# A two-layer decoder trunk on one core: more products on zeros, another order for the first rounding, and the small inputs on ScalarE's queue

## The chip, the cores and the metric

The kernel runs on one core of one Trainium2 chip. The metric is the device time of one execution in microseconds (us); the figure for a kernel is the median of its runs. One execution of the kernel before was also taken with the hardware profiler, and every view below is of that execution.

A core has TensorE (PE in the profile, with PEld for its weight loads), VectorE (DVE), ScalarE (ACT), GpSimd (POOL), and SyncE (SP), which here only issues transfers. Each engine runs its own instructions in the order of the program; an instruction whose operands are not ready holds up all that stand behind it on that engine.

## The reference, cut to what matters

```python
D_MODEL, SEQ, DEPTH, HEAD_DIM = 1024, 512, 2, 64
def fox_moba_layer(x, norm_g, w_in, ...):         # layer 0
    h = rms_norm(x, norm_g)
    proj = h @ w_in                               # 1024 x 4104 columns
    # split: q,k,v of 8 forgetting heads, their forget logits, q,k,v of 8 MoBA heads, gate
    out_a = fox_attention(...); out_b = moba_attention(...)
    mix = concatenate([out_a, out_b])
    return x + (mix * silu(gate)) @ w_out
def conformer_conv_layer(x, ...):                 # layer 1
    val, glu_gate, z = split(rms_norm(x, norm_g) @ w_in, 3)
    u = depthwise_causal_conv(val * sigmoid(glu_gate), width=31) + conv_b
    return x + (silu(layer_norm(u)) * silu(z)) @ w_out
```

All is in float32. Layer 0 starts with the product of the normalised tokens, 512 x 1024, with the columns of `l0_w_in`.

## The kernel before, in words

Products in float32 are made of three products of rounded operands: a tensor `a` is kept as `hi` (rounded to TensorE's fp32r) and `lo = a - hi`, and `a @ w` is `hi·whi + lo·whi + hi·wlo`. The tokens' two halves are `hhi` and `hlo`, the weights' `whi` and `wlo`. The weights come in 36 chunks of 256 columns (1 MB each); chunk `i` is loaded into one of two buffers `wst` by `fetch(i)` and rounded by `split(i)` (`split_w`, L162 to L179): `whi` by ScalarE (L173), `wlo` by VectorE or GpSimd (L177), each in four pieces of two of the eight contraction steps k. For chunk 0 GpSimd makes the first and third piece of `wlo`, VectorE the second and fourth.

The start of the kernel, in the order of the code:
- `small_parts` (L200) loads the small inputs of layer 0 (norm gains, rope tables, biases; 90 KB) in one transfer on SP's queue (L203) to the tile `parts`.
- SP then loads the first token tile of the transposed input (`xt`, 128 tokens, in two halves, L218), the four quarters of weight chunk 0 (L152), the other three token tiles, and the untransposed rows `xs` with the weight chunks 1 and 2 between and behind them.
- TensorE does `WARM` = 11 products on a tile of zeros, `idle` (L313), whose result is never read.
- For each token tile `t` and each half of its channels: VectorE multiplies by the norm's gain (`hn`, which shows as `v`, L328), ScalarE rounds that to `hhi` (L330), VectorE subtracts to get `hlo` (L331). After tile 0 the code calls `split(0)`.
- For each tile ScalarE squares `xs` and sums it (L337), VectorE scales the sum (`vv`, L339) and GpSimd takes the power, which gives `rinv` (L340): the norm's factor, applied when a product is read out (L386, L388). `spread_rinv` transposes `rinv` on TensorE (L345).
- Chunk 0 (`qk_chunk(0)`) is the first real product: 24 matmuls for each of four token tiles (L360), all `whi·hhi` first, then `whi·hlo`, then `wlo·hhi`. Tile 0 and 1 write the banks `mm`, tile 2 and 3 the banks `s`. Chunk 1 writes `mm`, `mm`, `st` and `o`; chunk 2 follows.

The code is not in the final order: a scheduler of the language simulates the program and orders the instructions of each engine by their simulated times. `tc.issue_after(x)` holds the instructions under it back, in that order, until `x` has been placed. So a change at the start can alter the order of everything behind it.

Of the kernel before, what the change touches and what calls it, by code (L numbers as in the profile page):

```python
# [57 lines left out]
def SPLIT_ENG(i, nc):  # L58

    if i in DMAS:  # L60
        return None
    return nc.gpsimd if i in PSPLIT else nc.vector
# [20 lines left out]
KO = 4  # L83
KORD = (6, 0, 1, 2, 4, 5, 7, 3)
SPR = 1
WARM = 11
WARM2 = 2
HP = None
HP1 = None
# [5 lines left out]
def tile_kernel(ctx: ExitStack, tc: tile.TileContext, x, xt, w, small0, small1, l1_norm, out):  # L95
# [7 lines left out]
    V, A, G, T, SY = nc.vector, nc.scalar, nc.gpsimd, nc.tensor, nc.sync  # L103
# [20 lines left out]
    def mmbank():  # L124
        turn[0] += 1
        return stbank() if l1p and turn[0] % 3 == 0 else bank("mm", 2)
# [7 lines left out]
    def bc_row(src, n, parts=P):  # L134
        return bass.AP(tensor=src.tensor, offset=src.offset, ap=[[0, parts], [1, n]])
# [19 lines left out]
    def split_w(w, ring, eng, parts, cast):  # L155
        st, n = w
        if ring == "late":
            lo = l1p[0].tile([P, KC * WC], F32R, tag="gh", name="lo", bufs=1)
            lo = lo.rearrange("p (k n) -> p k n", k=KC)
            A.activation(lo, st, AF.Copy, scale=-1.0)  # L160
            G.dma_start(lo.bitcast(F32), st, accum_op=ALU.add)
            return None, lo  # L162
        if ring == "main":
            hi, lo = flat(main, F32R, "whi", n, 2), flat(main, F32R, "wlo", n, 2)
        else:
            hi, lo = (flat(l1p[0], F32R, "wx", n, 4, WC) for _ in range(2))
        m = KC // parts
        if cast:
            G.dma_start(hi, st)
        for k in range(0, KC, m):  # L170
            ks = slice(k, k + m)
            if not cast:
                A.activation(hi[:, ks], st[:, ks], AF.Copy)  # L173
            if eng is None:
                A.activation(lo[:, ks], st[:, ks], AF.Copy, scale=-1.0)
            else:
                (V if eng is G and parts == 4 and k % 4 and V0 else eng).tensor_tensor(lo[:, ks], st[:, ks], hi[:, ks].bitcast(F32), op=ALU.subtract)  # L177
        if eng is None:
            G.dma_start(lo.bitcast(F32), st, accum_op=ALU.add)  # L179
        return hi, lo  # L180
# [16 lines left out]
    tab = so.tile([P, 2, NT, 4, 16], F32, name="tab")  # L197


    def small_parts(src, sizes, pool):  # L200
        n = sum(m for _, m in sizes)
        t = pool.tile([P, n], F32, name="parts")
        SY.dma_start(t, src)  # L203
        r, o = {}, 0
        for name, m in sizes:
            r[name] = t[:, o:o + m]
            o += m
        return r

    parts0 = small_parts(small0, SIZES0, consts)  # L210
    xts = []
    for t in range(NT):
# [18 lines left out]
    def split(i):  # L231
        if i < len(wsrc):
            wts[i] = split_w(raw.pop(i), rings[i], SPLIT_ENG(i, nc), APARTS if i in DMAS else 4 if i == 0 or 17 <= i < 24 else WPARTS, i in CAST)
# [77 lines left out]
    pw = mmbank()  # L311
    for _ in range(WARM):
        T.matmul(pw, idle[:, :P], idle, start=True, stop=True)  # L313
# [9 lines left out]
    for t in range(NT):  # L323
        hn = v0[:, (t % 2) * KC * P:(t % 2 + 1) * KC * P].rearrange("p (k t) -> p k t", k=KC)
        ts = slice(t * P, (t + 1) * P)
        for h in range(2):
            ks = slice(h * 4, h * 4 + 4)
            V.tensor_tensor(hn[:, ks], xts[t][:, ks], gcol[:, ks, None].to_broadcast([P, 4, P]),  # L328
                            op=ALU.mult)
            hp[2 * t + h] = hpart = A.activation(hhi[:, ks, ts], hn[:, ks], AF.Copy)  # L330
            V.tensor_tensor(hlo[:, ks, ts], hn[:, ks], hhi[:, ks, ts].bitcast(F32),  # L331
                            op=ALU.subtract)
        if t == 0:
            split(0)
    for t in range(NT):
        with tc.issue_after(hp[JO[t]].ins):
            A.activation(xs[t], xs[t], AF.Square, accum_out=ssx[:, t:t + 1])  # L337
# [347 lines left out]
    l1 = ctx.enter_context(tc.tile_pool(name="l1", bufs=1, reuse_waits="tile"))  # L685
# [4 lines left out]
    gh = l1.tile([P, 2, D], F32, tag="gh", name="gh", bufs=1)  # L690
    grow1, hn1 = gh[:, 0], gh[:, 1]
    SY.dma_start(grow1, bc_row(l1_norm, D))
    parts1 = small_parts(small1, SIZES1, l1)
    cw = parts1["conv_w"].rearrange("p (k w) -> p k w", k=KC)
    V.tensor_scalar(cw, cw, 0.5, None, op0=ALU.mult)
    cbias, lng, lnb = parts1["conv_b"], parts1["ln_g"], parts1["ln_b"]
# [427 lines left out]
SIZES1 = (("conv_b", KC), ("ln_g", KC), ("ln_b", KC), ("conv_w", KC * CONV))  # L1124
# [62 lines left out]
```

## Time and profile before

| | us |
|---|---|
| median of 3 runs | 524.99 (523.45 to 526.51) |
| the profiled execution, its own time | 525.7 |
| its span, first to last instruction | 523.9 |
| PE busy | 505.9 (97% of the span) |
| DVE, ACT, POOL busy | 375.8, 329.8, 232.3 |

The mean granted clock of TensorE was 0.984. A matmul's end is modelled in the trace and its start is not, so a PE that is shown as busy may still be slowed: the count of matmuls in a stretch and the clock tell how fast it ran. Rows of a timeline have start, duration, engine, line, operation, operands and count, and in brackets the idle time before and what ended it. Rows of a table of stretches have, for each stretch, the busy time of PE, PEld, DVE, ACT and POOL with the number of instructions, the granted clock, the share of the 16 DMA engines in use and GB/s.

### The profile page before, as it was taken

The page shows a single profiled execution, that of the slowest core. Times are in us where ns is not written, and L with a number is a line of the kernel's source. Part 1 is how long each engine was busy: PE and PEld are TensorE (multiplying, and loading weights), DVE is VectorE, ACT ScalarE, POOL GpSimd, SP SyncE. Part 2 cuts the span into 40 slices and gives each one's busy share as a digit, 9 for nine tenths or more (in the row PEclk, how much of TensorE's full clock was granted, in tenths as well). Part 3 has the DMA queues.
Part 4 walks back from the last instruction along what each step waited for, and adds up shares of the span by engine and source line. Part 5 has one row for each costly group of instructions (what it writes and reads, how often), then busy time and mean ns, then how long its engine had stood idle before and what let it go on. Part 6 is the DMA issues. An engine that isn't in the chain of part 4 may idle for free.

```text
span 523.9 us, 9734 instructions
## 1 busy us (share of the span) xinstructions
PE 505.9 (97%) x3683; PEld 462.0 (88%) x3683; DVE 375.8 (72%) x788; ACT 329.8 (63%) x668; POOL 232.3 (44%) x255
## 2 busy tenths in 40 slices
PE   6999999999999999999999999999999999779997
PEld 3999998987889988788779999999999887559997
DVE  6856577856565587586696256999999997778741
ACT  3846687876555785576374735998686755478230
POOL 4166545010323143223202113879998875777200
PEclk8999999999999999999999999999999999879999
DMA  7742222202122233303219578488999799962111
GB/s 264 306 180 83 81 81 102 76 30 82 61 102 81 81 125 99 138 10 114 102 41 398 124 213 233 89 210 290 230 305 255 203 261 314 265 171 101 41 49 43
DMA packets 16566, 79.05 MB, mean 151 GB/s; under 512 B 1988, under 2 KB 4352, under 8 KB 8712
## 3 DMA queue, kind: packets, MB, share of 16 engines
q1 hardware_dynamic: 12776, 51.17, 26.8%
q0 software_dynamic: 3744, 27.26, 21.7%
q8 instruction: 29, 0.48, 0.4%
q14 instruction: 17, 0.14, 0.1%
HBM read 50.07 MB, written 2.14 MB: 100 GB/s over the span
## 4 chain that ended last, share of the span: by engine, by line
PE 72%; DMA 12%; DVE 5%; ACT 5%; POOL 3%; issue 2%; SPq 0%; POOLq 0%; ACTq 0%
PE mm L360 30%; DMA wst<-in_w_dram 7%; PE mm L369 6%; PE mm L370 6%; PE mm L371 6%; PE st L360 4%; PE o L602 3%; PE tp L525 3%; POOL pacc L775 2%; PE o L360 2%; PE s L509 2%; DMA lo<-wst 2%; PE s L511 2%; DMA wlo<-wst 2%; DMA wx<-wst 2%
## 5 line engine op out<-in xcount | busy, mean ns | idle before, releaser
L775 POOL TENSOR_TENSOR pacc<-pacc,tm 128x256 f32<-128x256 f32 (+1 forms) x125 | 120.2, 982 | 16.3 <-ACT tm L774 10.5
L765 DVE SCALAR_TENSOR_TENSOR s<-u,parts,s 128x256 f32<-128x256 f32 (+1 forms) x211 | 108.2, 571 | 0.5
L360 PE MATMUL mm<-whi,hhi 128*128 128x256 f32 (+1 forms) x352 | 100.2, 292 | 3.1 <-ACT hhi L330 2.9
L360 PE MATMUL mm<-whi,hlo 128*128 128x256 f32 (+1 forms) x352 | 99.4, 289 | 0.0
L360 PE MATMUL mm<-wlo,hhi 128*128 128x256 f32 (+1 forms) x352 | 99.0, 289 | 0.0
L774 ACT ACTIVATE tm<-u,parts 128x256 f32<-128x256 f32 (+1 forms) x125 | 66.2, 571 | 14.7 <-POOL pacc L775 14.2
L360 PEld LDWEIGHTS mm<-whi,hhi 128*128 128x128 f32 x352 | 66.9, 193 | 4.7 <-ACT hhi L330 3.4
L360 PEld LDWEIGHTS mm<-whi,hlo 128*128 128x128 f32 x352 | 66.7, 193 | 0.2
L360 PEld LDWEIGHTS mm<-wlo,hhi 128*128 128x128 f32 x352 | 66.6, 193 | 0.2
L173 ACT ACTIVATE whi<-wst 128x512 fp32r<-128x512 f32 (+2 forms) x77 | 49.3, 707 | 8.8 <-DMA wst<-in_w_dram 7.8
L522 ACT ACTIVATE p<-p,nm 128x128 f32<-128x128 f32 (+3 forms) x64 | 35.8, 559 | 26.9 <-DVE nm L521 26.3
L517 POOL TENSOR_TENSOR cb<-cb,mask 128x128 f32<-128x128 f32 x32 | 15.4, 485 | 77.4 <-DVE nm L521 48.8
L177 POOL TENSOR_TENSOR wlo<-wst,whi 128x512 fp32r<-128x512 f32 (+1 forms) x22 | 31.0, 1417 | 38.3 <-ACT whi L173 38.3
L177 DVE TENSOR_TENSOR wlo<-wst,whi 128x512 fp32r<-128x512 f32 (+1 forms) x50 | 40.4, 840 | 9.9 <-ACT whi L173 9.8
L369 PE MATMUL mm<-nhi,wx 128*128 128x256 f32 (+1 forms) x104 | 33.8, 325 | 0.0
L371 PE MATMUL mm<-nhi,wx 128*128 128x256 f32 (+1 forms) x104 | 32.9, 316 | 0.0
L370 PE MATMUL mm<-nlo,wx 128*128 128x256 f32 (+1 forms) x104 | 32.8, 316 | 0.0
L370 PE MATMUL mm<-nlo,whi 128*128 128x256 f32 (+1 forms) x104 | 31.9, 307 | 0.0
L369 PE MATMUL mm<-nhi,whi 128*128 128x256 f32 (+1 forms) x104 | 31.8, 307 | 0.0
L371 PE MATMUL mm<-nhi,wlo 128*128 128x256 f32 (+1 forms) x104 | 31.7, 306 | 0.0
L395 POOL TENSOR_TENSOR rq<-vq,mhalf 128x16 f32<-128x16 f32 x8 | 26.2, 3281 | 5.0 <-DVE vq L393 4.9
L525 PE MATMUL tp<-identf,p 128*128 128x128 f32 x160 | 28.1, 275 | 0.4 <-ACT pt L533 0.3
(292 smaller groups left out, 1434.8 us busy)
## 6 DMA issues: line engine op xcount, KB each, us to landing
wst<-in_w_dram SPq DMA_DIRECT2D x33, 1024.0 KB, 5.2
wx<-wst POOLq DMA_DIRECT2D x13, 1024.0 KB, 7.9
wlo<-wst POOLq DMA_DIRECT2D x8, 1024.0 KB, 8.9
whi<-wst POOLq DMA_DIRECT2D x3, 1024.0 KB, 5.9
wst<-in_w_dram SPq DMA_DIRECT2D x2, 1040.0 KB, 4.7
xs<-in_x_dram SPq DMA_DIRECT2D x4, 512.0 KB, 9.4
cb<-cdram SPq DMA_DIRECT2D x8, 256.0 KB, 3.7
x<-in_x_dram SPq DMA_DIRECT2D x4, 512.0 KB, 7.2
```

Source lines behind the costliest of these rows:

```text
L173: A.activation(hi[:, ks], st[:, ks], AF.Copy)
L177: (V if eng is G and parts == 4 and k % 4 and V0 else eng).tensor_tensor(lo[:, ks], st[:, ks], hi[:, ks].bitcast(F32), op=ALU.subtract)
L360: T.matmul(po, a[:, k, ts], b[:, k, :n], start=first and i == 0, stop=last and i == len(prods) - 1)
L369: T.matmul(po, whi[:, k, cs], a, start=k == 0, stop=False)
L370: T.matmul(po, whi[:, k, cs], b, start=False, stop=False)
L371: T.matmul(po, wlo[:, k, cs], a, start=False, stop=k == KC - 1)
L395: G.tensor_tensor(r, v, mhalf[:, :16].rearrange("p (t h) -> p t h", t=NT), op=ALU.pow)
L522: A.activation(p[:, :w], p[:, :w], AF.Exp, bias=nm, scale=-1.0, accum_out=sm[:, h, t:t + 1])
L525: T.transpose(tp[:, j * P:(j + 1) * P], p[:, j * P:(j + 1) * P], identf)
L765: V.scalar_tensor_tensor(acc[:, o], v, w, first[0][:, :n] if i == 1 else acc[:, o], op0=ALU.mult, op1=ALU.add)
L774: A.activation(tm[:, :n], v, AF.Copy, scale=w)
L775: G.tensor_tensor(pacc[:, o], pacc[:, o], tm[:, :n], op=ALU.add)
```

## The change

It has three parts. `WARM` goes from 11 to 22. `small_parts` issues on ScalarE's queue unless told otherwise, and layer 1's call names SP's queue, so only the load at the start moves. `split(0)` is held back until the second rounding of tile 0 has been placed.

```diff
-WARM = 11
+WARM = 22
...
-    def small_parts(src, sizes, pool):
+    def small_parts(src, sizes, pool, queue=None):
         n = sum(m for _, m in sizes)
         t = pool.tile([P, n], F32, name="parts")
-        SY.dma_start(t, src)
+        (A if queue is None else queue).dma_start(t, src)
...
         if t == 0:
-            split(0)
+            with tc.issue_after(hpart.ins):
+                split(0)
...
-    parts1 = small_parts(small1, SIZES1, l1)
+    parts1 = small_parts(small1, SIZES1, l1, SY)
```

The change adds one line, so lines behind L334 are one higher in the new kernel (L360 is L361).

ScalarE at the start, before:

```order
L260 ACT_TABLE_LOAD
L260 ACTIVATE first<-mhalf 128x1
L173 ACTIVATE whi<-wst 128x512
L330 ACTIVATE hhi<-v_75 128x4x128
L173 ACTIVATE whi<-wst 128x512
L330 ACTIVATE hhi<-v_75 128x4x128
L173 ACTIVATE whi<-wst 128x512 x2
```

and in the changed kernel:

```order
L203 DMA parts<-in_small_dram 128x180
L260 ACT_TABLE_LOAD
L260 ACTIVATE first<-mhalf 128x1
L330 ACTIVATE hhi<-v_75 128x4x128 x2
L173 ACTIVATE whi<-wst 128x512 x4
```

The transfer stands first, and both roundings of token tile 0 stand ahead of the four pieces of `whi`, where they alternated.

VectorE from the first residues on (`hlo` of the tokens, `wlo` of the weights, `v` the scaled tokens of the next tiles), before:

```order
L331 TENSOR_TENSOR hlo<-v_75,hhi 128x4x128
L177 TENSOR_TENSOR wlo<-wst,whi 128x512
L331 TENSOR_TENSOR hlo<-v_75,hhi 128x4x128
L177 TENSOR_TENSOR wlo<-wst,whi 128x512
L328 TENSOR_TENSOR v_75<-xt,parts 128x512 x4
L331 TENSOR_TENSOR hlo<-v_75,hhi 128x4x128 x3
```

and in the changed kernel:

```order
L331 TENSOR_TENSOR hlo<-v_75,hhi 128x4x128 x2
L177 TENSOR_TENSOR wlo<-wst,whi 128x512
L328 TENSOR_TENSOR v_75<-xt,parts 128x512 x2
L177 TENSOR_TENSOR wlo<-wst,whi 128x512
L331 TENSOR_TENSOR hlo<-v_75,hhi 128x4x128
L328 TENSOR_TENSOR v_75<-xt,parts 128x512 x2
```

Both residues of tile 0 now come first, and the two multiplications of token tile 1, which need its transfer, have moved ahead of VectorE's second piece of `wlo`.

TensorE where chunk 1 begins (with the numbers of the buffers: the first four outputs before are the banks of token tiles 0 to 3), before:

```order
L360 MATMUL mm_384<-whi_231,hhi_165 128x256
L360 MATMUL mm_412<-whi_231,hhi_165 128x256
L360 MATMUL st_440<-whi_231,hhi_165 128x256
L360 MATMUL o_468<-whi_231,hhi_165 128x256
L360 MATMUL mm_384<-wlo_232,hhi_165 128x256
L360 MATMUL mm_384<-whi_231,hlo_166 128x256
```

and in the changed kernel:

```order
L361 MATMUL mm_395<-whi_242,hhi_176 128x256
L361 MATMUL mm_423<-whi_242,hhi_176 128x256
L361 MATMUL mm_395<-wlo_243,hhi_176 128x256
L361 MATMUL mm_395<-whi_242,hlo_177 128x256
L361 MATMUL mm_395<-whi_242,hhi_176 128x256
```

The four token tiles advanced together before; now tile 0 and 1 go first and tile 2 and 3 follow later. With that the transposition of `rinv` (L345, now L346) stands 35 matmuls behind the first of chunk 1, where it stood 54 behind it, and the first matmul that needs GpSimd's second piece of chunk 2's `wlo` stands 98 behind it, where it stood 117. Further on, up to the end of the attention, products and attention steps are interleaved at other places on TensorE, VectorE and ScalarE, with the same instructions.

## The prediction

> **What bounds the kernel now.** First the page's head, the clock line and the shares of the chain that ended last, then one row of the table of stretches for the attention stage.
>
> ```profile
> span 523.9 us, 9734 instructions
> PEclk8999999999999999999999999999999999879999
> PE 72%; DMA 12%; DVE 5%; ACT 5%; POOL 3%; issue 2%; SPq 0%; POOLq 0%; ACTq 0%
> 60.00:262.00 202.00, 201.48 (x1422) 176.39 (x1421) 137.32 (x303) 133.82 (x314) 59.28 (x61) 1.00 0.24 83
> ```
>
> TensorE carries 72% of the chain, and between 60 and 262 us it is idle for 0.52 of 202 us. So a matmul that starts earlier at the front moves everything behind it until something else ends a wait. The clock line is below 9 in two places: the first slice, which the change touches, and one near the end. The chain's first pieces show what the front waits for:
>
> ```profile
> 2.12 5.51 DMA wst<-in_w_dram
> 7.65 0.63 ACT whi L173
> 8.28 0.52 ACT hhi L330
> ...
> 9.84 0.53 ACT whi L173
> 10.41 6.15 PE mm L360 x28
> ```
>
> The first weight quarter lands at 7.65, ScalarE rounds until 10.4, and from there TensorE sets the time. How fast it ran is in the products on zeros and in the starts of the groups of real ones:
>
> ```profile
> L313 PE MATMUL mm<-idle x11: 380/634/634, 1.4 to 5.6; 128*128 128x512 bf16 x11
> 1.44 4.51 PE L313 MATMUL mm<-idle 128*128 128x512 bf16 x11 [1.44 <-DVE idle L310]
> 8.85 1.32 PE L360 MATMUL mm<-whi,hhi 128*128 128x256 f32 x4 [2.90 <-ACT hhi L330]
> 15.24 1.32 PE L360 MATMUL mm<-whi,hhi 128*128 128x256 f32 x8
> 24.08 0.40 PE L360 MATMUL mm<-whi,hhi 128*128 128x256 f32 x2
> 38.02 0.28 PE L360 MATMUL mm<-wlo,hhi 128*128 128x256 f32 x1
> ```
>
> Ten of the eleven zero products take 634 ns and the last 380: the clock came up just as they ended, about 4.2 us after the first. They start (5.6 - 1.44)/10 = 0.42 us apart. Then TensorE is idle for 2.90 us. Token tile 0 (24 matmuls) takes from 8.85 to 15.24; chunk 1 begins at 24.08. From there to 38.02 stand 117 matmuls and one transposition, 0.119 us each: that is the full pace. Stretches cut at 3.41 us from the fall of the clock:
>
> ```profile
> 5.52:8.93 3.41, 0.52 (x3) 0.08 (x1) 1.19 (x11) 1.28 (x3) 0.57 (x1) 0.99 0.84 261
> 8.93:12.34 3.41, 3.17 (x12) 2.70 (x12) 3.41 (x3) 2.06 (x4) 2.17 (x2) 0.50 1.03 420
> 12.34:15.76 3.42, 3.42 (x17) 3.32 (x17) 3.42 (x7) 2.06 (x4) 0.00 (x0) 0.51 1.02 414
> 15.76:19.17 3.41, 3.41 (x31) 3.41 (x31) 3.41 (x8) 2.67 (x5) 0.00 (x0) 1.00 1.02 416
> 442.42:445.83 3.41, 2.48 (x11) 1.70 (x9) 0.15 (x1) 2.73 (x5) 2.92 (x5) 1.00 0.98 209
> 459.49:462.90 3.41, 1.12 (x5) 0.57 (x4) 0.26 (x2) 3.41 (x7) 3.03 (x5) 0.99 0.78 298
> 462.90:466.31 3.41, 2.11 (x9) 1.85 (x10) 3.41 (x5) 2.19 (x6) 3.10 (x5) 0.50 0.98 204
> 466.31:469.73 3.42, 3.34 (x9) 2.03 (x8) 3.28 (x7) 1.85 (x6) 3.19 (x5) 0.51 0.60 120
> ```
>
> The clock changes only at the cuts of this grid, 450 us apart as well. A stretch with 3 or 5 matmuls is followed by half clock, one with 11 is not; it comes back after a full stretch. So the whole front from 8.93 to 15.76 ran at half clock because of the idle 2.90 us.
>
> **More products on zeros.** At 0.42 us each until the clock rises at 5.6, the rest at half of that: 11 more by 0.21 = 2.3, so the 22 end near 8.2. In an execution whose grid lies otherwise the rise can come up to one stretch after the first full one, at the latest 1.44 + 2 x 3.41 = 8.3; then 16 take 0.42 and 6 take 0.21 and they end near 9.5. Data sets TensorE's pace until after 10 (next part), so the tail costs nothing. From the end of the zeros to 10.6 only six real matmuls can run, but the stretch that holds them goes on into dense work and has over 11, so by the rows above the clock stays.
>
> The Trainium skill (TensorE: Matmul & The Clock Gate, Part 1) says the gate watches a free-running window of 3413 ns, cold by default. The trace's grid agrees. The page adds that the cold count differs from run to run, so by it the half-clock end at 15.76 is one draw of a spread one window wide, and my term for it could be 1.7 us larger or smaller in another execution.
>
> **The transfer on ScalarE's queue, and the landing of the data.**
>
> ```profile
> 0.75 0.38 SPq L203 DMA_DIRECT2D parts<-in_small_dram  x1
> 1.19 0.89 SPq L218 DMA_DIRECT2D xt<-in_xt_dram  x2
> 1.50:2.50 1.00, 1.00 (x3) 0.37 (x4) 0.81 (x2) 0.72 (x2) 0.00 (x0) 1.00 0.43 113
> 10.00:15.00 5.00, 4.76 (x20) 4.34 (x20) 5.00 (x8) 2.30 (x5) 1.47 (x1) 0.50 1.03 419
> L152 SPq DMA_DIRECT2D wst<-in_w_dram x2: 432/432/432, 3.1 to 3.5; - x2
> DMA to landing us min/median/max: 6.8/6.8/6.8
> 6.09 1.88 SPq L243 DMA_DIRECT2D xs<-in_x_dram  x2
> xs<-in_x_dram SPq DMA_DIRECT2D x1, 512.0 KB, 9.4
> 10.38 0.63 ACT L173 ACTIVATE whi<-wst 128x512 fp32r<-128x512 f32 x1
> ```
>
> SP's transfers all move up by 1.19 - 0.75 = 0.44 us. The landing moves up by no more than that and by no less than nothing: the 16 DMA engines were only 43% in use from 1.5 to 2.5, so part of it is real. I take 0.3, since more than half of that first stretch was free. ScalarE's 0.4 us for issuing lies ahead of its table load and is covered by its idle time until 7.65.
>
> The fourth weight quarter landed at 3.5 + 6.8 = 10.3, when the fourth `whi` began (10.38): the weights, not ScalarE's alternation, paced that engine. Rounding tile 0 first therefore gains nothing by itself on `whi`, which ends at 11.0 - 0.3 = 10.7. Token tile 1 is the next 512 KB: 0.524 MB by 419 GB/s = 1.25 us, so 11.6 before and 11.3 after. The same sum with three more such tiles gives 15.3 for the first `xs`, and the trace has 6.09 + 9.4 = 15.5, so the estimate stands.
>
> The Trainium skill (DMA: Bandwidth & Descriptors, Issuing engines are not separate DMA queues) says a second issuing engine saves only the time of issuing, usually small. With none of it my sum loses 0.3.
>
> **The order.** What is left of the front is VectorE's queue.
>
> ```profile
> 12.38 0.68 DVE L177 TENSOR_TENSOR wlo<-wst,whi 128x512 fp32r<-128x512 f32 x1
> 12.98 2.48 DVE L328 TENSOR_TENSOR v<-xt,parts 128x512 f32<-128x512 f32 x4
> 20.14 0.69 DVE L331 TENSOR_TENSOR hlo<-v,hhi 128x512 fp32r<-128x512 f32 x1 [0.33 <-ACT hhi L330]
> 22.02 2.19 ACT L173 ACTIVATE whi<-wst 128x512 fp32r<-128x512 f32 x4
> 26.54 0.55 POOL L340 TENSOR_TENSOR rinv<-vv,mhalf 128x1 f32<-128x1 f32 x1 [0.48 <-DVE vv L339]
> 33.20 1.29 POOL L177 TENSOR_TENSOR wlo<-wst,whi 128x512 fp32r<-128x512 f32 x1
> ```
>
> Four multiplications in 2.48 us are 0.60 apart. In the new order the two of token tile 1 stand ahead of the last piece of `wlo`, so that piece waits for a transfer that it does not need: it begins at 11.3 + 1.2 = 12.5 and ends at 13.2, no earlier than before (13.06). TensorE, at full pace: the last `whi` at 10.7, two matmuls, eight with `hlo`, six with `wlo`, 16 x 0.12 = 1.9, makes 12.6; it waits 0.6 for the last piece, and tile 1 begins at 13.2 + 0.24 = 13.4 instead of 15.24: **1.8 us earlier**. This is where the clock's gain is cut.
>
> Behind it, VectorE has 13 more of these operations for chunk 0, from 12.38 to 20.83 before and from 11.3 now, 1.1 earlier, and 72 matmuls x 0.12 = 8.6 and some 0.2 of waits for `hhi` of tile 2 end at 22.25: chunk 1 begins 24.08 - 22.25 = 1.8 earlier. What ScalarE and GpSimd owe it moves by VectorE's 1.1 alone: the first `whi` piece of chunk 1 is there at 21.5 (needed at 22.25), the last `rinv` at 27.09 - 1.1 = 26.0, with its transposition due at 22.25 + 35 x 0.119 = 26.4, and GpSimd's last `wlo` of chunk 2 at 34.49 - 1.1 = 33.4, due at 22.25 + 98 x 0.119 = 33.9. All three are in time, the last two by under 0.5 us where there were over 3. Further on the attention is reordered, but TensorE stood full there, so I put it at nothing, within 0.5 either way.
>
> **The sum**: -1.8 us. The profiled execution's own time is 525.7 with a span of 523.9, so it would be 523.9; the median of runs, 524.99, lies 0.7 below it, which gives **523.2** for the median. That is 0.34%; 0.5% (2.6 us) is about what a measurement of this kernel can tell from no change.
>
> **The rivals.**
> Late covers: nothing is gained on landing, and the transposition of `rinv` or GpSimd's `wlo`, with margins of 0.4 and 0.5 us, stop TensorE. For it: VectorE's new wait for token tile 1, and two margins as small as my error. Against: 0.44 of issue time is really taken off SP. With 0.3 later landing and a chain that does not move, 27.09 against 26.4 and 34.49 against 33.9 leave 1.1 or less: 524.2.
> The late clock: the half clock from 462.90 to 469.73 comes from a stretch that the grid cuts so that it has 5 matmuls. Moved by 1.8 us against the grid, the same idle time is shared by two stretches, and the clock may stay. 18 matmuls in 6.8 us at half clock could take some 2 us less; VectorE is busy throughout, which speaks against the full 3.4. Then 1.8 + 2.0: 521.2. Against it: where the grid lies may be chance in both kernels' medians.
> Slower: TensorE works in order, so if the clock does not rise until the zeros are done, 22 x 0.42 end at 10.8, two us behind the first data (8.85). Then the real products start two later and at half clock: 24 x 0.24 makes tile 1 begin at 16.6, 1.3 later: 526.3. It decides if the clock comes up after 10; the row with 380 ns at 5.6 is against it.
> That the change does nothing to the clock (it falls again in the sparse microseconds up to 10.6) would leave the half pace and some 0.3 for the landing: 524.7. The stretch with 11 matmuls speaks against it.
>
> **How the numbers follow.** My forecast 0.48, late covers 0.22, late clock 0.20, clock falls again 0.05, slower 0.05. The range reaches from the late clock to past the late covers and the falling clock, with the 0.5 of the reordering: 520.9 to 525.4. Faster by over 0.5% takes the late clock and a little of the forecast's lower tail: 0.25; slower by over 0.5% needs the slow rival and more beside it: 0.05; the same is 0.70.
>
> **What would show it.** The zeros end near 8 to 9.5 and the granted clock stays at 1.00 from 8.9 on; `whi`'s last piece ends near 10.7; VectorE waits for `xt` near 9.5 to 11.3; token tile 1 begins near 13.4, chunk 1 near 22.3, and TensorE does not stop at `rinv`'s transposition. The prediction is wrong if the clock falls in the front, if landing moves by more than 0.44, or if the attention's new order opens waits on TensorE.

## The result, and the profile after

| | before | changed | ratio, 95% interval |
|---|---|---|---|
| first comparison, median of 9 and 9 runs | 524.69 us | 522.22 us (521.41 to 523.6) | 0.9943 [0.992, 0.9967] |
| second, 30 and 12 runs | 524.51 us | 522.22 us | 0.9958 [0.9942, 0.9975] |

The change gains 2.3 to 2.5 us; 1.8 was forecast. One run of the kernel with the rounding order alone took 551.98 us at a mean clock of 0.845; this slow run is left out of the ratios and of the account by late clock below. The profiled execution of the changed kernel took 522.39 us. First its page's head with the clock line and the shares of the chain that ended last:

```profile
span 520.6 us, 9754 instructions
PEclk9999999999999999999999999999999999989999
PE 70%; DMA 8%; POOL 7%; ACT 6%; DVE 4%; issue 3%; SPq 0%; POOLq 0%; ACTq 0%
```

TensorE carries 70% of the chain, where it was 72%. The 8 in the first slice of the clock has become a 9; the weak place near the end is still there. The front, from the timeline (start, length, engine and line; in brackets the idle time ahead and what ended it):

```profile
0.74 0.41 ACTq L203 DMA_DIRECT2D parts<-in_small_dram  x1
0.75 0.85 SPq L218 DMA_DIRECT2D xt<-in_xt_dram  x2
1.45 7.86 PE L313 MATMUL mm<-idle 128*128 128x512 bf16 x22 [1.45 <-DVE idle L310]
6.79 1.91 ACT L173 ACTIVATE whi<-wst 128x512 fp32r<-128x512 f32 x3 [0.19 <-DMA wst<-in_w_dram]
8.96 1.45 PE L361 MATMUL mm<-whi,hhi 128*128 128x256 f32 x8
9.21 0.63 ACT L173 ACTIVATE whi<-wst 128x512 fp32r<-128x512 f32 x1 [0.51 <-DMA wst<-in_w_dram]
10.68 1.29 DVE L328 TENSOR_TENSOR v<-xt,parts 128x512 f32<-128x512 f32 x2 [1.25 <-DMA xt<-in_xt_dram]
11.88 0.68 DVE L177 TENSOR_TENSOR wlo<-wst,whi 128x512 fp32r<-128x512 f32 x1
12.62 0.50 PE L361 MATMUL mm<-wlo,hhi 128*128 128x256 f32 x2 [0.55 <-DVE wlo L177]
12.96 1.11 PE L361 MATMUL mm<-whi,hhi 128*128 128x256 f32 x8
21.84 0.40 PE L361 MATMUL mm<-whi,hhi 128*128 128x256 f32 x2
```

The zeros end at 9.3 and the real products stand right behind them; the 2.90 us of idle time are gone. The last piece of `whi` begins at 9.21, VectorE waits until 10.68 for token tile 1, and TensorE then waits 0.55 us for the last piece of `wlo`, as the prediction had it. Chunk 1 begins at 21.84, where it began at 24.08.

Two stretches of each kernel, before and then changed (columns: stretch, length, busy time and count of PE, PEld, DVE, ACT and POOL, granted clock, DMA share, GB/s):

```profile
0.00:24.00 24.00, 19.42 (x107) 15.84 (x108) 18.26 (x42) 14.05 (x26) 7.62 (x17) 0.86 0.84 310
440.00:480.00 40.00, 32.28 (x164) 26.23 (x162) 29.75 (x72) 27.92 (x62) 29.25 (x40) 0.87 0.74 208
```

```profile
0.00:24.00 24.00, 22.01 (x137) 16.86 (x138) 18.78 (x44) 16.35 (x29) 8.96 (x18) 1.00 0.83 310
440.00:480.00 40.00, 30.98 (x177) 25.86 (x176) 29.18 (x67) 27.28 (x63) 30.43 (x41) 0.96 0.67 181
```

The front's clock is whole. In the late stretch 0.13 of 40 us was lacking before, which is three stretches of 3.41 us at half clock, and 0.04 is lacking now, which is one. So the two profiles differ late as well. The end of layer 0 is marked by the first residue of the last stage, again before and then changed:

```profile
L680 DVE TENSOR_TENSOR mlo<-ot,mhi x8: 686/689/693, 264.9 to 274.2; 128x512 fp32r<-128x512 f32 x8
```

```profile
L681 DVE TENSOR_TENSOR mlo<-ot,mhi x8: 684/685/693, 262.8 to 272.1; 128x512 fp32r<-128x512 f32 x8
```

The 2.2 us of the front arrive there nearly whole, 2.1. The profiles' spans differ by 3.3, and the other 1.2 come in layer 1. Whether the change earned those is asked below.

### The profile page after: what moved, and what is told of

Same layout as the page of the kernel before. It is cut to its first block, busy times and chain, and to the rows that moved or that the text cites. A ratio compares the mean times of both kernels' runs of the same rounds, so it can differ in the third digit from the quotient of the medians.

```text
span 520.6 us, 9754 instructions
## 1 busy us (share of the span) xinstructions
PE 503.7 (97%) x3694; PEld 459.9 (88%) x3694; DVE 373.0 (72%) x788; ACT 329.1 (63%) x668; POOL 232.6 (45%) x255
## 4 chain that ended last, share of the span: by engine, by line
PE 70%; DMA 8%; POOL 7%; ACT 6%; DVE 4%; issue 3%; SPq 0%; POOLq 0%; ACTq 0%
PE mm L361 29%; POOL pacc L776 6%; PE mm L370 6%; PE mm L371 6%; PE mm L372 6%; DMA wst<-in_w_dram 5%; PE st L361 4%; PE o L603 3%; PE tp L526 3%; PE o L361 2%; PE s L510 2%; PE s L512 2%; DMA wlo<-wst 1%; DMA xt<-in_xt_dram 1%; PE s L361 1%
## 5 line engine op out<-in xcount | busy, mean ns | idle before, releaser
L776 POOL TENSOR_TENSOR pacc<-pacc,tm 128x256 f32<-128x256 f32 (+1 forms) x125 | 120.7, 986 | 15.8 <-ACT tm L775 10.1
L361 PE MATMUL mm<-wlo,hhi 128*128 128x256 f32 (+1 forms) x352 | 98.7, 287 | 0.8 <-DVE wlo L177 0.5
L361 PE MATMUL mm<-whi,hhi 128*128 128x256 f32 (+1 forms) x352 | 98.4, 287 | 0.0
L361 PE MATMUL mm<-whi,hlo 128*128 128x256 f32 (+1 forms) x352 | 98.3, 286 | 0.0
L361 PEld LDWEIGHTS mm<-wlo,hhi 128*128 128x128 f32 x352 | 65.8, 190 | 2.0 <-DVE wlo L177 0.8
L361 PEld LDWEIGHTS mm<-whi,hhi 128*128 128x128 f32 x352 | 65.6, 189 | 0.7 <-issue 0.2
L361 PEld LDWEIGHTS mm<-whi,hlo 128*128 128x128 f32 x352 | 65.9, 190 | 0.2
L370 PE MATMUL mm<-nhi,wx 128*128 128x256 f32 (+1 forms) x104 | 33.0, 318 | 0.0
L372 PE MATMUL mm<-nhi,wx 128*128 128x256 f32 (+1 forms) x104 | 31.9, 307 | 0.0
```

The lines of the kernel that those rows point to most:

```text
L361: T.matmul(po, a[:, k, ts], b[:, k, :n], start=first and i == 0, stop=last and i == len(prods) - 1)
L370: T.matmul(po, whi[:, k, cs], a, start=k == 0, stop=False)
L372: T.matmul(po, wlo[:, k, cs], a, start=False, stop=k == KC - 1)
L776: G.tensor_tensor(pacc[:, o], pacc[:, o], tm[:, :n], op=ALU.add)
```

## The experiments

Landmarks of the profiled executions, in us from the span's start; the ratio is to the kernel before on the same chip.

| kernel | clock 0 to 24 us | first `whi` piece | chunk 1 begins | end of layer 0 | median | ratio, 95% interval |
|---|---|---|---|---|---|---|
| before | 0.86 | 7.65 | 24.08 | 264.9 | 524.69 | |
| changed | 1.00 | 6.79 | 21.84 | 262.8 | 522.22 | 0.9943 [0.992, 0.9967] |
| changed, again (r_after) | 1.00 | 6.41 | 21.48 | 262.4 | 522.22 | 0.9958 [0.9942, 0.9975] |
| zeros alone (e1) | 1.00 | 7.13 | 22.93 | 264.1 | 524.39 | 0.9993 [0.9973, 1.0012] |
| queue alone (e2) | 0.86 | 6.04 | 22.89 | 263.7 | 524.59 | 0.9997 [0.9975, 1.0018] |
| rounding alone (e3) | 0.86 | 8.67 | 23.64 | 265.3 | 525.68 | 1.0016 [0.9997, 1.0035] |
| changed without the zeros (e4) | 0.86 | 6.79 | 23.60 | 265.2 | 524.62 | 1.0012 [0.9993, 1.0032] |
| changed without the rounding (e9) | 1.00 | 6.40 | 22.29 | 263.6 | 522.67 | 0.9957 [0.9937, 0.9977] |

**One part at a time.** Theory: each part shows its own landmark, and the zeros carry the gain. Rival: the landing carries it.

```
-WARM = 11
+WARM = 22
```

> The kernel before with 22 products on zeros and nothing else. Clock theory (the idle 2.9 us before the first real product cost the half clock from 8.9 to 15.8): the clock stays at 1.00 from the end of the zeros on, the landing is as before (last whi piece begins near 10.4), token tile 1 begins near 13.3 instead of 15.24 and chunk 1 near 22.6 instead of 24.08: 1.5 us less, ratio 0.997. Landing theory (what counts is that the transfers come a microsecond earlier): the engines behind the transfers bind anyway, chunk 1 begins at 23.5 or later, ratio 0.999 to 1.000.

The clock stayed up and chunk 1 began 1.15 us earlier, which the landing theory had excluded, and layer 0 ended 0.8 earlier. The median did not move by an amount that can be told, and the interval leaves out the 0.997 of the clock theory, if only just.

```
-    def small_parts(src, sizes, pool):
+    def small_parts(src, sizes, pool, queue=None):
-        SY.dma_start(t, src)
+        (A if queue is None else queue).dma_start(t, src)
-    parts1 = small_parts(small1, SIZES1, l1)
+    parts1 = small_parts(small1, SIZES1, l1, SY)
```

> The kernel before with the small inputs on ScalarE's queue and nothing else. Landing theory: the first weight quarter lands near 6.8 instead of 7.65, the last near 9.2 instead of 10.35, token tile 1 near 10.7; chunk 1 begins a microsecond or more earlier, ratio 0.998. Clock theory: the data is there as early, but TensorE still idles after the zeros, runs at half clock until the grid's end and gains 0.5 us at most, ratio 0.999. If the landing moves by the 0.44 us of issue time alone, the microsecond seen with all three parts was chance of that execution.

The first weight piece was there at 6.04, 1.6 us earlier, far more than the 0.44 us of issuing. TensorE still fell to half clock (0.86), as the clock theory said, but chunk 1 began and layer 0 ended 1.2 us earlier in this profile, where that theory allowed 0.5. The median stayed.

```
         if t == 0:
-            split(0)
+            with tc.issue_after(hpart.ins):
+                split(0)
```

> The kernel before with token tile 0 rounded ahead of the weights and nothing else. Both theories: the weights pace ScalarE, so the last whi piece ends within 0.2 us of 11.0; the wlo piece behind one of token tile 1's multiplications begins near 12.4 as before; no change in the time, ratio 0.999 to 1.001. A theory in which the order is what gains would have 0.5 us or more here.

Here the landing was late (8.67, with the last piece of `whi` ending at 11.3), though the transfers are those of the kernel before, and TensorE stood idle for 3.97 us behind the zeros. Chunk 1 began 0.44 earlier all the same, but the end of layer 0 came 0.4 later. By itself this part brings nothing.

**The whole change again, and without one part.**

> The changed kernel once more, beside the others of this set. The small inputs' transfer on its own queue: weights land as in the changed kernel (first piece of whi from 6.0 to 6.8, last from 9.0 to 9.3). Layer 0 theory (the gain is all in layer 0, about 2.1 us at the first residue of mlo, and layer 1 adds chance of 1.5 us either way): mlo begins near 262.8, ratio 0.996 to 0.994. If layer 1 gained by itself, its stretch from mlo to the last output would again be near 255.0 us as in the changed kernel's profile, where the others had 254.9 to 257.7.

The gain repeats, with the same median, and layer 0 ended at 262.4, 2.5 us earlier than before. Layer 1 took 254.8 us, near the 255.0 that the expectation names as the sign of a gain of its own. That doesn't decide it, because the kernels with the rounding alone (e3) and with the small transfer second (e7) took 254.9 there; the late clock is looked at below.

```
-WARM = 22
+WARM = 11
```

> The changed kernel with 11 products on zeros again (transfer and rounding order kept). Clock theory: TensorE idles from about 6 to 8 us, the clock falls or never came up, chunk 1 begins 1.0 us or more later than 21.84 and mlo near 264; ratio 0.998 to 1.000. Landing theory: the data is as early as in the changed kernel, chunk 1 begins within 0.4 us of 21.84 and the ratio is that of the changed kernel.

With eleven zeros and everything else of the change, the gain is gone. The stretches show why (5.5 to 9, 9 to 12.4 and 12.4 to 15.8 us; first this kernel, then the changed one):

```profile
5.50:9.00 3.50, 1.56 (x7) 0.68 (x5) 2.84 (x12) 2.94 (x5) 3.08 (x6) 0.98 0.98 301
9.00:12.40 3.40, 2.74 (x11) 2.45 (x12) 1.80 (x4) 1.31 (x3) 1.52 (x1) 0.50 1.02 417
12.40:15.80 3.40, 3.40 (x18) 3.40 (x17) 3.40 (x6) 2.23 (x4) 0.00 (x0) 0.51 1.04 427
```

```profile
5.50:9.00 3.50, 3.50 (x14) 1.39 (x12) 3.05 (x12) 2.97 (x5) 3.19 (x6) 1.00 1.01 324
9.00:12.40 3.40, 3.08 (x24) 2.76 (x22) 2.15 (x4) 1.63 (x3) 1.57 (x1) 1.00 1.03 420
12.40:15.80 3.40, 3.18 (x24) 3.03 (x25) 3.40 (x7) 2.23 (x4) 0.00 (x0) 1.00 1.03 427
```

The data land about as early, but a first stretch with seven matmuls is followed by half clock, and TensorE does 11 and 18 matmuls at half clock where it does 24 and 24 at full. The half clock lasts from about 8.9 to 15.7 us, two stretches of 3.41. The Trainium skill (TensorE: Matmul & The Clock Gate, Part 1) has a window of 3413 ns behind this, and these stretches agree with it.

The changed kernel without the `issue_after` ahead of `split(0)`:

> The changed kernel without the new rounding order (22 products on zeros and the small inputs on ScalarE's queue). The rounding order alone gained nothing and cost 0.4 us at mlo. If it is of no use beside the other two either, mlo begins within 0.2 us of 262.6. If it pays once the clock and the landing are early: VectorE makes the second hlo of token tile 0 beside GpSimd's wlo (1.77 us instead of 0.69) and token tile 1's multiplications begin near 11.9 instead of 10.7, chunk 1 begins near 22.3 instead of 21.5 to 21.8, and mlo near 263.1.

Chunk 1 begins 0.45 later than in the changed kernel (0.8 later than in its second execution), at the 22.3 of the second branch, and layer 0 ends at 263.6, 0.5 later than that branch said. The ratios of the two, 0.9957 and 0.9943 or 0.9958, can't be told apart.

**What landing gained, and from what.** Theory: SP issues everything 0.44 us earlier and that is all. Rival: the small transfer, 128 rows of 720 bytes, slows what stands behind it in its queue. In this kernel it stays on SP, but behind the two halves of token tile 0 (zeros and rounding as in the change):

```
-    parts0 = small_parts(small0, SIZES0, consts)
...
+    parts0 = small_parts(small0, SIZES0, consts)
```

> The changed kernel with the small inputs back on SP's queue, behind the first token tile's two halves instead of ahead of them; the other engines' instructions are in the changed kernel's order. Own-queue theory (small packets hold up what stands behind them in the same queue): the weights stand behind the small inputs again, 3 to 5 us move 200 to 240 GB/s as in the three kernels with them on SP, where the five with them on ScalarE's queue moved 329 to 347, the first weight quarter lands at 7.1 or later, token tile 1 at 11.5 or later and mlo begins 0.8 us or more behind 262.6. Issue-time theory (it is only being first that costs): token tile 0 comes as early, the weights 0.4 us later than in the changed kernel, 3 to 5 us move over 300 GB/s, mlo begins within 0.4 us of 262.6.

The stretch from 3 to 5 us, first before, then changed, then this kernel:

```profile
3.00:5.00 2.00, 2.00 (x6) 0.76 (x5) 1.12 (x5) 0.00 (x0) 1.80 (x6) 1.00 0.84 239
```

```profile
3.00:5.00 2.00, 2.00 (x6) 0.76 (x5) 1.50 (x5) 0.00 (x0) 0.58 (x2) 1.00 1.00 341
```

```profile
3.00:5.00 2.00, 2.00 (x6) 0.76 (x5) 0.86 (x3) 0.00 (x0) 0.00 (x0) 1.00 0.81 195
```

With the small transfer on SP's queue, first or second, the 16 DMA engines are 81 to 84% busy and move 195 to 239 GB/s in these two microseconds; with it on ScalarE's queue they are full and move 341. The same stretch gave 237 and 198 in the two other profiles with it first on SP, and 326 to 347 in the others that have it on ScalarE's queue. This is what the rival asks for, but the stretch by itself overstates it: up to 3 us the three profiles with the transfer first on SP had moved more, 0.25 to 0.29 MB, than the eight with it on ScalarE's queue, 0.17 to 0.22 MB. The view of the DMA packets from 0 to 8 us says what it adds up to, before and then changed:

```profile
DMA packets 840, 1.37 MB, mean 171 GB/s; under 512 B 89, under 2 KB 217, under 8 KB 840
```

```profile
DMA packets 1016, 1.76 MB, mean 220 GB/s; under 512 B 104, under 2 KB 232, under 8 KB 1016
```

0.39 MB more by 8 us is 0.93 us of transfers at the 420 GB/s of the next stretch; the 0.44 us of issuing would be half of that. But these two executions lie at the ends of their groups. The same view from 0 to 12 us, before, changed and this kernel:

```profile
DMA packets 1364, 3.00 MB, mean 250 GB/s; under 512 B 143, under 2 KB 271, under 8 KB 1364
```

```profile
DMA packets 1471, 3.39 MB, mean 282 GB/s; under 512 B 155, under 2 KB 283, under 8 KB 1471
```

```profile
DMA packets 1405, 3.15 MB, mean 263 GB/s; under 512 B 146, under 2 KB 274, under 8 KB 1405
```

The three profiles with the transfer first on SP have 3.00 to 3.13 MB by then and the eight with it on ScalarE's queue 3.24 to 3.41, in the mean 0.27 MB apart: 0.64 us at 420 GB/s, of which issuing explains 0.44. This kernel issues its weights 0.48 us later than the changed one, and the mean of the eight less 0.48 us at 420 GB/s is 3.14 MB, what it has. The 0.2 us left over in the others is less than executions with the same transfers differ by: the last piece of `whi` ended at 11.0 before, at 10.4 with the zeros alone and at 11.3 with the rounding alone. So a gain of the issue time is shown; that the small rows hold up their queue beyond it is suggested by the stretch of 3 to 5 us, but not shown. A confound remains in this kernel: token tile 0's multiplication needs the small inputs too, and began at 6.37 (4.44 in the changed kernel), so its late chunk 1 (23.55) and its ratio of 0.9965 [0.9941, 0.9989] are not the queue's rate alone. How the packets of one queue hold each other up, the records don't show.

**The wait for `wlo`.** The prediction has the clock's gain cut by VectorE's new order. Here VectorE does the last piece of `wlo` first and then waits for token tile 1:

```
+    lastw = [None]
...
-                (V if eng is G and parts == 4 and k % 4 and V0 else eng).tensor_tensor(lo[:, ks], st[:, ks], hi[:, ks].bitcast(F32), op=ALU.subtract)
+                lastw[0] = (V if eng is G and parts == 4 and k % 4 and V0 else eng).tensor_tensor(lo[:, ks], st[:, ks], hi[:, ks].bitcast(F32), op=ALU.subtract)
...
-            V.tensor_tensor(hn[:, ks], xts[t][:, ks], gcol[:, ks, None].to_broadcast([P, 4, P]),
-                            op=ALU.mult)
+            with tc.issue_after(lastw[0].ins) if t == 1 else nullcontext():
+                V.tensor_tensor(hn[:, ks], xts[t][:, ks], gcol[:, ks, None].to_broadcast([P, 4, P]),
+                                op=ALU.mult)
```

> The changed kernel with VectorE's last piece of chunk 0's wlo held ahead of the first multiplication of token tile 1. In the changed kernel VectorE stood idle for 1.25 us up to the landing of token tile 1 at 10.7 while that piece was ready to be made, and TensorE then waited 0.55 us for it. If that wait is on the path, token tile 0 ends near 12.2, token tile 1 begins near 12.4 instead of 12.96 and 0.5 us is gained on the changed kernel (ratio to the kernel before 0.9935 where the changed kernel has 0.9943). If hhi of token tile 1 (second half ready near 12.6) binds instead, the gain is 0.2 us or less.

TensorE's waits up to 75 us (total, times, longest), first the changed kernel, then this one:

```profile
PE mm L361 <- DVE wlo L177: 0.5, 1, 0.5
PE mm L361 <- POOL wlo L177: 0.3, 1, 0.3
```

```profile
PE mm L364 <- POOL wlo L179: 0.7, 1, 0.7
PE mm L364 <- ACT hhi L333: 0.2, 1, 0.2
```

The wait of 0.5 is gone, tile 1 begins at 12.35 and chunk 1 at 21.39, but other waits have grown by 0.6, and layer 0 ends at 262.8, as without the edit. The median was 523.85 us, ratio 0.9978 [0.9955, 1.0], where 0.9935 was expected. Its time by the account at the end of this section is 1.3 +- 0.7 us longer than the changed kernel's, for which I have no row. The next bound is further on: chunk 3's first piece.

```profile
43.79 2.19 ACT L173 ACTIVATE whi<-wst 128x512 fp32r<-128x512 f32 x4 [2.45 <-PE mm L361]
44.50 6.39 POOL L177 TENSOR_TENSOR wlo<-wst,whi 128x512 fp32r<-128x512 f32 x4 [8.40 <-ACT whi L173]
45.83 0.39 PE L361 MATMUL mm<-wlo,hhi 128*128 128x256 f32 x1 [0.27 <-POOL wlo L177]
```

In the changed kernel (these rows) ScalarE may round chunk 3's weights only after a matmul has ended at 43.79; 0.6 us of rounding and 1.3 us of GpSimd later the first `wlo` is there, and TensorE has waited 0.27. In the kernel with the edit the same rounding begins at 43.86, and TensorE waits there longer:

```profile
45.90 0.39 PE L364 MATMUL mm<-wlo,hhi 128*128 128x256 f32 x1 [0.74 <-POOL wlo L179]
```

What TensorE had won by chunk 1 was gone at this wait.

Then chunk 2's `wlo` as well from VectorE, on top of that edit:

```
-PSPLIT = (0, 2, 3, 4, 5, 6, 8, 9, 10, 14, 16, 18)
+PSPLIT = (0, 3, 4, 5, 6, 8, 9, 10, 14, 16, 18)
```

> The changed kernel with VectorE's wlo piece ahead of token tile 1 (as before) and chunk 2's wlo made by VectorE alone. Theory: GpSimd's second piece of chunk 2's wlo, which stands behind a power of 3.4 us, is what took back the 0.45 us that the earlier order had gained: TensorE waited 0.7 us for it, where the changed kernel had 0.3 and the kernel before none. Without it that wait is gone and mlo begins near 262.1 instead of 262.8; ratio 0.7 us below that of the changed kernel's. Rival: the next wait behind it takes the place, and mlo stays within 0.2 us of 262.8.

The expectation had the place wrong: the 0.7 us was the wait for chunk 3's first `wlo` at 45.90, not for chunk 2's second piece. With the edit no wait for GpSimd is left. Layer 0 ends at 262.5, between the theory's 262.1 and the rival's 262.8. Chunk 1 began late in this execution (22.11), and from there to the end of layer 0 it takes 240.4 us, the least of all twelve profiles (241.0 in the changed kernel, 241.4 without this edit). The median was 521.79 us, ratio 0.9951 [0.9933, 0.9969]. It is the lowest median here, though not apart from the changed kernel's.

**More zeros than the cover holds.**

```
-WARM = 22
+WARM = 36
```

> The changed kernel with 36 products on zeros. If the zeros are free only up to the landing: 14 more at 0.21 us end 3.0 us later, near 12.3 instead of 9.3; token tile 0's 24 products then take 2.9 us from there, token tile 1 begins near 15.2 instead of 12.96, and chunk 1 near 23.8 instead of 21.84, since TensorE then runs 72 products without a wait. Rival: VectorE's queue binds chunk 0 anyway (its last hlo ends near 18.9) and takes up half of the delay: chunk 1 near 22.8.

```profile
12.48 0.50 PE L361 MATMUL mm<-wlo,hhi 128*128 128x256 f32 x2 [0.24 <-DVE wlo L177]
14.35 1.83 PE L361 MATMUL s<-whi,hhi 128*128 128x256 f32 x8 [1.36 <-ACT hhi L330]
15.98 2.59 PE L313 MATMUL mm<-idle 128*128 128x512 bf16 x6
```

It was slower, 527.72 us, ratio 1.0051 [1.0027, 1.0075], but not by the mechanism meant. Thirty zeros stood ahead, and the 24 products of tile 0 end by 13 as in the changed kernel. The other six went in at 15.98, between real products, tile 2 was taken ahead of tile 1, with a wait of 1.36 us, and chunk 1 began at 26.08. So it shows what a disturbed order costs, and not where the cover of the zeros ends.

**The late clock.** Layer 1 took 256.3 us before (from 264.9 to the last output's issue at 521.2) and 255.0 in the changed kernel, with the same instructions. Is that the forecast's rival, a shift against the clock's grid? Every timed run comes with its mean granted clock. One stretch of 3.41 us at half clock takes 0.5 x 3.41 / 523 = 0.0033 off it, so the clock counts such stretches. All four profiles with eleven zeros have two of them in the front, and the profiles with 22 zeros have none; what is left over is late. Sorted so, all runs whose clock was listed (88 of the kernel before, 21 of the changed one):

| stretches at half clock, late | before: runs, median | changed: runs, median | difference |
|---|---|---|---|
| 1 | 47, 524.29 us | 5, 521.76 us | 2.53 |
| 2 | 25, 524.77 us | 13, 522.22 us | 2.55 |
| 3 | 12, 526.67 us | 3, 524.11 us | 2.56 |

(Four runs of before had one, two or six in all.) At equal late clock the gain is 2.5 to 2.6 us each time. The changed kernel doesn't have fewer of them: 1.9 in the mean against 3.5 - 2 = 1.5. The two profiles happened to be a run with three (before, 525.7 us) and one with one (changed), which can account for their 1.2 us in layer 1. So the shift against the grid gave nothing that these counts show. This count takes the front's two stretches for given in the runs without a profile, and that is an assumption.

The same account, one straight line through all these runs and those of the other kernels (36 zeros left out) with a price for each late stretch (1.01 +- 0.16 us; 3.41 us of nothing but matmuls at half pace would lose 1.7) and a shift for each kernel, tells the parts apart better than the medians do (+- is the 95% interval):

| kernel | shift from before, us, at equal late clock |
|---|---|
| zeros alone | -1.02 +- 0.58 |
| queue alone | -0.42 +- 0.57 |
| rounding alone | +0.42 +- 0.59 |
| changed without the zeros | +0.01 +- 0.57 |
| changed without the rounding | -2.11 +- 0.57 |
| small transfer second on SP (e7) | -1.86 +- 0.58 |
| `wlo` first (e5) | -1.62 +- 0.57 |
| changed | -2.89 +- 0.45 |
| `wlo` first, chunk 2's from VectorE (e8) | -3.26 +- 0.73 |

The kernels were run in three sets on three chips, and the runs of before on the last one, with e7 and the kernel without the rounding, are about 0.4 us slower. Compared on their own chip these two come out at -2.1 and -2.4 +- 0.7, and the second set of the changed kernel at -2.6 +- 0.7.

## Why the prediction was right, and where its size was off

- **The clock: right.** The zeros end at 9.3 (8 to 9.5 was said), the clock is 1.00 from 5.5 to 15.8, and 22 zeros in place of 11 are the condition of the whole gain: -2.89 us with them, +0.01 without. With eleven zeros and early data the critical stretch has seven matmuls, and the clock falls behind it. The prediction allowed this term 1.7 us either way from execution to execution; in the four profiles with eleven zeros the half clock ends between 14.4 and 15.8 us but lasts two stretches each time.
- **The landing: the mis-sized term.** The step was "the landing moves up by no more than that [0.44] and by no less than nothing", taken as 0.3, with token tile 1 at 11.3 and `whi` ended at 10.7. Measured in the two profiles: tile 1 at 10.68 and 10.31, `whi` ended at 9.84 and 9.7. That is 0.9 to 1.3 us earlier than the 11.6 estimated and the 11.0 measured for before. A landing moved by more than 0.44 was a named sign of being wrong, and this term was. Some of the size is chance of the executions: over all profiles the data by 12 us is 0.64 us ahead and `whi` ended 1.0 earlier (9.94 against 10.90 in the mean). Issue time gives 0.44 of it; whether the small rows themselves hold up the queue is not settled. The rule of the Trainium skill (DMA: Bandwidth & Descriptors, Issuing engines are not separate DMA queues), that a second issuer saves only issue time, gave the same bound; the runs lie above it, but not clear of their spread.
- **The rounding order and VectorE's wait: right in place and size.** TensorE waits 0.55 us for the last `wlo` (0.6 was said), tile 1 begins at 12.96 instead of 13.4, since its data came 0.6 earlier than forecast, and chunk 1 follows 8.88 later (8.85). "Gains nothing by itself" holds for the part alone (+0.42 +- 0.59); with the others it is worth 2.89 - 2.11 = 0.8 +- 0.7 at equal late clock, but only 0.2 +- 0.9 when each is compared with before on its own chip. Whether it helps there is not settled.
- **The margins: right, and the next wait stood elsewhere.** The last `rinv` comes in time for its transposition at 26.0 although TensorE is 0.4 earlier than forecast, and GpSimd's second piece of chunk 2 ends at 32.55, due at 21.84 + 98 x 0.119 = 33.5. The wait that did open is for chunk 3's first `wlo` at 45.8, 0.27 us, in the reordered part that was put at nothing. "Within 0.5 either way" holds: from chunk 1 to the end of layer 0 it takes 241.0 us (240.8 before). That bound is not safe for every order: two others here took 0.8 to 0.9 more, with a wait of 0.7 us in the attention.
- **The late clock: rightly not forecast.** The table by late stretches speaks against the rival that gave 521.2: the changed kernel has no fewer of them, as far as the count of the front holds.
- **Slower: not seen.** The zeros did outlast the first data: the first piece of `whi` was rounded at 7.4 and the first real product began at 8.96. But their pace had doubled near 7.5, within what the term for the zeros allowed, and TensorE still reached the last `wlo` 0.55 us too early, so the delay cost nothing. Where it would begin to cost was not found, since the kernel with 36 zeros didn't put them there.

So the sum comes out as 2.2 us at chunk 1 in place of 1.8, and the rest is the spread of the medians. The median of 522.22 lies 1.0 below the forecast 523.2; 0.3 to 0.5 of that is the starting point, since the three first runs of before (524.99) were above the later ones (524.69 and 524.51).

## What to carry to other kernels

Products on zeros that bridge the wait for the first data can keep the first real products from half clock if they reach up to them; look for the stretch with too few matmuls and fill that one. Earlier data and an earlier order together brought nothing here while the clock fell behind them (+0.01 +- 0.57), so parts that look empty alone should be tried together. A small transfer at the head of the queue costs the large ones behind it at least its issue time (0.44 us here), so put it where they don't stand behind it.

## What the runs showed of the hardware that was not expected

- With a transfer of 90 KB in rows of 720 bytes on the queue of the large ones, 195 to 239 GB/s were moved from 3 to 5 us, against 326 to 347 with it on another queue. By 12 us the difference is 0.27 MB, 0.64 us, little more than the 0.44 us of issuing.
- The number of half-clock stretches of the same kernel differs from run to run (3 to 5 in 84 of 88 runs of before), and goes with part of the spread of its time: 524.29 us with three, 526.67 with five.
- The moment at which the zeros double their pace differs as well: about 5.6 us in the profile of before, 7.5 in that of the changed kernel (an estimate from 22 starts between 1.45 and 8.9 us, 0.42 apart and then 0.21), with zeros of 634 ns until then and 379 behind. The column of the granted clock doesn't show this: it reads 1.00 from 3 to 5 us.

```profile
L313 PE MATMUL mm<-idle x22: 379/634/634, 1.4 to 8.9; 128*128 128x512 bf16 x22
```
